# Sliding-window extraction on one core: who loads which half of the channels, and what goes through a staging buffer

## The chip, the cores and the metric

The kernel runs on one core of a Trainium2 chip. The metric is the time of one execution on the device, in microseconds (us); the median of the runs counts. The profile shows one execution of its own, which is named beside its span below.

## The reference

The input x is an array of 16 x 64 x 64 x 64 32-bit floats (batch b, channel c, row, column). From each image, windows of 8 x 8 are cut at a stride of 4, and all are written out, window after window:

```
n_h = (h - window_size) // stride + 1      # 15
n_w = (w - window_size) // stride + 1      # 15
for i in range(n_h):
    for j in range(n_w):
        result[:, i, j] = x[:, :, i*4 : i*4+8, j*4 : j*4+8]
```

Nothing is computed; 16.78 MB are read and, since windows overlap, 58.98 MB are written (16 x 15 x 15 windows of 64 channels x 64 values, 16 KB each).

## The kernel before

**Layout.** The whole input is held in the tile L (line 49). A partition holds one channel half (ch, 32 of the 64 channels), one image b and one quarter q of the rows (16 rows): p = ch x 64 + b x 4 + q, 128 KB each. Images come in two groups, y = 0 (b 0 to 7) and y = 1 (b 8 to 15), so a channel half and a group are 32 partitions. "Lower half" means ch = 0, partitions 0 to 63; "upper half" is ch = 1.

**Loads.** `load` (line 56) brings channels c0 to c1 of one ch, y and q: 8 partitions, every fourth one, with a run of 4 KB per channel. The first FC = 4 channels of each half do not come this way. They are staged: for each ch and q one DMA (line 112) of 16 partitions and 256 KB goes to S[ch], a view of partitions 32 to 95 of the output buffers G2 and G3, which are free at that time. ScalarE's queue issues the four DMAs of the lower half, SP's queue the four of the upper half. Copies at line 126 then bring them to their places in L: two on ScalarE for the lower half, two on VectorE for the upper half, 32 partitions x 4096 elements each. The rest is loaded directly, in the loop at line 114, which goes over y and q (8 steps): in the first six steps SP loads channels 8 to 32 of the lower half (768 KB) and GpSimd channels 4 to 8 (128 KB); in the last two GpSimd loads channels 4 to 32 (896 KB) alone; in all eight GpSimd loads channels 4 to 32 of the upper half (896 KB). That is 16 loads by GpSimd and 6 by SP.

**Output.** There are four output buffers of 128 x 16 KB, taken by turns. Each is filled by copies from L (ScalarE and VectorE; some on VectorE are shuffles with an identity or a next-partition mask), then stored by GpSimd with an indirect DMA of one 16 KB row per partition (`scatter`, line 137). Row numbers come from small index tiles (idx, idx_lo, idx_hi, idx_y0, idx_y1); idx_lo and idx_hi let 16 of the 128 rows fall out of bounds, and those are skipped. There are 29 such stores, and 2 plain ones of SP at the end (line 245).

**Order.** The first three buffers (`part`, line 189) need only y = 0: eight copies each of 32 partitions x 2048 elements, three on ScalarE and five on VectorE, four that read each channel half. Then `part` for y = 1 and `unit` (line 204) follow. A framework derives the waits from which parts of a tile each instruction touches, and may reorder instructions of an engine by its own estimates. It has eight semaphores for the DMAs that SP and ScalarE issue and eight for those of GpSimd; the ninth DMA of either kind waits until the first has landed, and so on.

Of the kernel before, what the change touches and what calls it, by code (L numbers as in the profile page):

```python
# [10 lines left out]
def kernel(  # L11
# [7 lines left out]
    nc = tc.nc  # L19
    P = nc.NUM_PARTITIONS  # L20

    B, C, H, W = x.shape
    Bo, NH, NW, Co, WSo, WSo2 = out.shape
    WS = int(window_size)
# [3 lines left out]
    f32 = mybir.dt.float32  # L28
    i32 = mybir.dt.int32
    ALU = mybir.AluOpType  # L30
    CH = 2
    HQ = P // (B * CH)
    CL = C // CH
    RB = H // HQ
# [3 lines left out]
    HP = P // CH  # L38
    YB = 8
    NY = B // YB  # L40
    QP = YB * HQ
# [4 lines left out]
    gpool = ctx.enter_context(tc.tile_pool(name="gpool", bufs=1))  # L46


    L = lpool.tile([P, CL, RB, W], f32)
# [1 line left out]

    SMALL, HWP = 4, 6

    def load(eng, ch, y, q, c0, c1):
        p0 = ch * HP + y * QP + q
        eng.dma_start(out=L[p0 : p0 + QP - HQ + 1 : HQ, c0:c1, :, :], in_=x_v[ch, y, q, :, c0:c1, :])  # L58
# [43 lines left out]


    NG = 4
    G = [gpool.tile([P, C, WS, WS], f32, name=f"G{n}") for n in range(NG)]
    FC = C * WS * WS // (RB * W)
    S = [g.rearrange("p c r w -> p (c r w)").rearrange("p (c r w) -> p c r w", c=FC, r=RB) for g in G[NG - CH :]]
    x_b = x.rearrange("b (ch cl) (hq r) w -> ch hq b cl (r w)", ch=CH, hq=HQ)
    for ch in range(CH):
        for q in range(HQ):  # L110
            s = S[ch][QP + q : QP + q + (B - 1) * HQ + 1 : HQ]
            (nc.scalar, nc.sync)[ch].dma_start(out=s, in_=x_b[ch, q, :, 0:FC, :])

    for y in range(NY):
        for q in range(HQ):
            hw = y * HQ + q < HWP
            if hw:
                load(nc.sync, 0, y, q, FC + SMALL, CL)
            load(nc.gpsimd, 0, y, q, FC, FC + SMALL if hw else CL)
            load(nc.gpsimd, 1, y, q, FC, CL)  # L120

    for y in range(NY):
        for ch in range(CH):
            f = slice(QP + y * QP, QP + (y + 1) * QP)
            d = slice(ch * HP + y * QP, ch * HP + (y + 1) * QP)
            (nc.scalar.copy, nc.vector.tensor_copy)[ch](out=L[d, 0:FC, :, :], in_=S[ch][f])  # L126

    o_v = out.rearrange("b i j c r w -> (b i j) (c r w)")
    nxt = [min(p + 1, 31) for p in range(32)]

    o_q = out.rearrange("b i j c r w -> i j b (c r w)")

# [27 lines left out]
                copy(out=g[d, cs, 0:ST, :], in_=L[f, :, s * ST : RB, cols])  # L160
                nc.vector.stream_shuffle(out=g[d, cs, ST:WS, :], in_=L[f, :, 0:ST, cols], mask=nxt)  # L161

    act, dve = nc.scalar.copy, nc.vector.tensor_copy
    same = list(range(32))


    def shf(out, in_):
        nc.vector.stream_shuffle(out=out, in_=in_, mask=same)  # L168

    def split(k, other):  # L170
        def both(out, in_):
# [3 lines left out]
        return both  # L175

    mix = split(CL // 4, shf)


# [4 lines left out]
    def tile_():  # L184
        nonlocal at
        at += 1
        return G[(at - 1) % NG]

# [15 lines left out]
    def unit(j, s, copies=(shf, mix)):  # L204
        nonlocal crossed
        g = tile_()
        if s == 0:
            fill(g, 0, 0, j, 0, HP, (act, copies[0]))
            fill(g, 1, 1, j, 0, HP, (act, copies[1]))
            scatter(g, idx, j, s)  # L210
        else:

            turn = 1 - crossed % 2
            crossed += 1
            fill(g, turn, s, j, 0, HP, (act, act))
            fill(g, 1 - turn, s + 1, j, 0, HP, (shf, mix))
            scatter(g, (idx_hi, idx_lo)[turn], j, s)
# [17 lines left out]
    for s in range(2):  # L235
        g = tile_()
        cols = slice(j * ST, j * ST + WS)
        for y in range(NY):
            d = slice(QP + y * QP, QP + (y + 1) * QP)
            for ch in range(CH):  # L240
                f = slice(ch * HP + y * QP, ch * HP + (y + 1) * QP)
# [39 lines left out]
```

## Time and profile before

| | |
|---|---|
| median of 3 runs | 187.62 us (187.61 to 187.77) |
| profiled execution | 187.89 us, its span 186.1 us |
| VectorE, ScalarE, GpSimd busy | 146.8, 146.5, 47.7 us |
| DMA mean | 407 GB/s, 75.81 MB |
| HBM read, written | 16.78 MB, 62.91 MB by the instructions' own account |
| staging DMAs issued | 0.7 to 3.6 us, landed 8.0 to 8.7 us (median) after issue |
| first copy into an output buffer | ScalarE 28.47 us, VectorE 28.49 us |
| first store issued, last | 42.14 us, 175.3 us |

In the profile's page, DMA digits give the mean busy share of the 16 DMA engines in 40 slices (a 9 is 90% or more). Queue q0 is GpSimd's (software), q1 is SP's and q10 is ScalarE's (hardware). A queue's row has its packets, its MB and the time that its packets took as a share of the 16 engines' time in the window. In rows in order of time the first number is the start, the second the duration, both in us; what stands in brackets is the idle time before and what ended it. POOL is GpSimd, ACT ScalarE, DVE VectorE.

### The profile page before, as it was taken

The numbers are of one execution on the slowest core, as the hardware profiler recorded it, in microseconds if no ns is written. First come the engines' busy times: TensorE is split into PE (matmuls) and PEld (weight loads), VectorE is DVE, ScalarE is ACT, GpSimd is POOL, SyncE is SP. The second block draws the span as 40 slices with busy tenths as digits, with TensorE's granted clock in tenths as the row PEclk, the third lists the DMA queues.
The fourth block names the chain that finished last, engine by engine and source line by source line (L and its number), as shares of the span: only waits on it lengthen the run. The fifth ranks groups of instructions, "written<-read, shape, count | busy, mean of one in ns | idle before, by whom it ended". The sixth has DMA issues, their size and how long they took to land.

```text
span 186.1 us, 575 instructions
## 1 busy us (share of the span) xinstructions
DVE 146.8 (79%) x205; ACT 146.5 (79%) x96; POOL 47.7 (26%) x50
## 2 busy tenths in 40 slices
DVE  5045008999998969799999999999999999998600
ACT  0069108997999989988899999998998899999600
POOL 7405222006335341422222222222222222223000
DMA  5999999999999999999999999999999999999994
GB/s 165 359 402 403 399 401 400 381 385 424 433 440 423 431 433 430 433 430 433 424 435 419 433 426 423 433 412 433 398 444 396 444 419 409 440 409 433 409 447 204
DMA packets 11300, 75.81 MB, mean 407 GB/s; under 512 B 3600, under 2 KB 3600, under 8 KB 7696
## 3 DMA queue, kind: packets, MB, share of 16 engines
q0 software_dynamic: 9296, 66.86, 86.6%
q1 hardware_dynamic: 1680, 7.86, 10.6%
q10 hardware_dynamic: 320, 1.05, 1.8%
q14 instruction: 4, 0.03, 0.0%
HBM read 16.78 MB, written 62.91 MB: 428 GB/s over the span
## 4 chain that ended last, share of the span: by engine, by line
DMA 41%; DVE 37%; issue 8%; ACT 5%; POOL 2%; ACTq 1%; POOLq 0%; DVEq 0%; PEldq 0%
DVE G L168 16%; DMA out_dram<-G,idx 14%; DMA out_dram<-G,idx_y 13%; DMA L<-in_x_dram 13%; DVE G L161 11%; DVE G L196 10%; ACT G L243 3%; POOL L L58 2%; ACT G L158 1%; ACT G L172 1%; ACTq L276 0%; DVE G L158 0%; POOLq L138 0%; POOL pi L69 0%; POOL out_dram L138 0%
## 5 line engine op out<-in xcount | busy, mean ns | idle before, releaser
L158 ACT COPY G<-L 64x2048 f32<-64x2048 f32 x46 | 87.2, 1896 | 5.8 <-DMA out_dram<-G,idx 3.7
L168 DVE STREAM_SHUFFLE G<-L 64x1024 f32<-64x1024 f32 (+4 forms) x39 | 53.0, 1358 | 1.2
L196 DVE COPY G<-L 32x2048 f32<-32x2048 f32 x30 | 36.6, 1220 | 14.9 <-DMA L<-in_x_dram 12.1
L196 ACT COPY G<-L 32x2048 f32<-32x2048 f32 x18 | 33.9, 1896 | 11.5 <-DMA L<-in_x_dram 10.4
L161 DVE STREAM_SHUFFLE G<-L 64x1024 f32<-64x1024 f32 x30 | 38.4, 1280 | 0.0
L138 POOL DMA_INDIRECT out_dram<-G,idx_y x6 | 10.7, 1776 | 26.7 <-DVE G L196 16.3
L58 POOL DMA_DIRECT2D L<-in_x_dram x16 | 11.9, 760 | 19.5 <-DMA L<-in_x_dram 19.0
L138 POOL DMA_INDIRECT out_dram<-G,idx_lo x8 | 7.7, 963 | 30.9 <-DVE G L161 12.0
L138 POOL DMA_INDIRECT out_dram<-G,idx x8 | 10.4, 1295 | 18.1 <-ACT G L158 9.3
L138 POOL DMA_INDIRECT out_dram<-G,idx_hi x7 | 6.7, 962 | 26.6 <-DVE G L161 19.0
L126 DVE COPY L<-G 32x4096 f32<-32x4096 f32 x2 | 4.6, 2284 | 8.2 <-DMA G<-in_x_dram 8.2
L172 ACT COPY G<-L 64x256 f32<-64x256 f32 (+2 forms) x21 | 10.2, 484 | 0.5
L126 ACT ACT_TABLE_LOAD x1 | 1.3, 1283 | 10.8 <-DMA G<-in_x_dram 10.8
L158 DVE COPY G<-L 64x2048 f32<-64x2048 f32 x6 | 7.3, 1222 | 0.2
L243 DVE COPY G<-L 32x1280 f32<-32x1280 f32 x8 | 6.5, 818 | 0.9 <-DMA out_dram<-G,idx_hi 0.8
L126 ACT COPY L<-G 32x4096 f32<-32x4096 f32 x2 | 7.2, 3604 | 0.0
L243 ACT COPY G<-L 32x768 f32<-32x768 f32 x8 | 6.6, 829 | 0.1
L168 DVE LOAD_MASK_SELECT G<-L x39 | 0.3, 8 | 1.4 <-DMA out_dram<-G,idx_y 1.0
L72 DVE TENSOR_SCALAR tb<-pi 128x1 int32<-128x1 int32 x1 | 0.2, 153 | 1.0 <-POOL pi L69 1.0
L173 DVE COPY G<-L 64x1280 f32<-64x1280 f32 x1 | 0.9, 874 | 0.0
L78 DVE TENSOR_TENSOR th<-tc,tq 128x1 int32<-128x1 int32 x2 | 0.3, 156 | 0.0
L75 DVE TENSOR_SCALAR th<-tc 128x1 int32<-128x1 int32 x2 | 0.3, 154 | 0.0
(21 smaller groups left out, 3.0 us busy)
## 6 DMA issues: line engine op xcount, KB each, us to landing
L<-in_x_dram POOLq DMA_DIRECT2D x10, 896.0 KB, 19.3
L<-in_x_dram SPq DMA_DIRECT2D x6, 768.0 KB
out_dram<-G SPq DMA_DIRECT2D x2, 1024.0 KB, 10.2
G<-in_x_dram ACTq DMA_DIRECT2D x4, 256.0 KB, 8.0
G<-in_x_dram SPq DMA_DIRECT2D x4, 256.0 KB, 8.7
L<-in_x_dram POOLq DMA_DIRECT2D x6, 128.0 KB, 18.2
out_dram<-G,idx POOLq DMA_INDIRECT x8, 13.2
out_dram<-G,idx_lo POOLq DMA_INDIRECT x8, 10.6
```

The lines of the kernel that those rows point to most:

```text
L58: eng.dma_start(out=L[p0 : p0 + QP - HQ + 1 : HQ, c0:c1, :, :], in_=x_v[ch, y, q, :, c0:c1, :])
L75: nc.vector.tensor_scalar(out=d[:, :], in0=a[:, :], scalar1=float(m), scalar2=None, op0=ALU.mult)
L78: nc.vector.tensor_tensor(out=d[:, :], in0=a[:, :], in1=b[:, :], op=op)
L126: (nc.scalar.copy, nc.vector.tensor_copy)[ch](out=L[d, 0:FC, :, :], in_=S[ch][f])
L138: st = nc.gpsimd.indirect_dma_start(out=o_v, out_offset=bass.IndirectOffsetOnAxis(ap=ix[:, 0:1], axis=0), in_=g.rearrange("p c r w -> p (c ...
L158: copy(out=g[d, cs, :, :], in_=L[f, :, s * ST : s * ST + WS, cols])
L161: nc.vector.stream_shuffle(out=g[d, cs, ST:WS, :], in_=L[f, :, 0:ST, cols], mask=nxt)
L168: nc.vector.stream_shuffle(out=out, in_=in_, mask=same)
L172: act(out=out[:, 0:k], in_=in_[:, 0:k])
L173: other(out=out[:, k:], in_=in_[:, k:])
L196: (act if (2 * d + ch) % 3 == 0 else dve)(out=g[d * QP : (d + 1) * QP, ch * CL : (ch + 1) * CL, :, :], in_=L[f : f + QP, :, s * ST : s * S ...
L243: copy(out=g[d, ch * CL + c0 : ch * CL + c1, :, :], in_=L[f, c0:c1, s * ST : s * ST + WS, cols])
```

## The change

The four output buffers become views of one tile GG, so that the staging buffer S can be one run over the last two of them: 8 channels of one half instead of 4 of each. Only the lower half is staged, by ScalarE's queue alone, four DMAs of 512 KB (16 partitions, 8 channels). SP loads channels 8 to 32 of the lower half directly in all eight steps; the first two steps are cut into two loads of 12 channels. GpSimd loads only the upper half, all 32 channels, in each step 4 channels (128 KB) and then 28 (896 KB). The staging copies become two: ScalarE's for y = 0 and a VectorE shuffle with the identity mask for y = 1, 32 partitions x 8192 elements each. The helpers `act`, `dve`, `same` and `shf` move up.

```
-    SMALL, HWP = 4, 6
+    SMALL, TWICE = 4, 2
...
-    G = [gpool.tile([P, C, WS, WS], f32, name=f"G{n}") for n in range(NG)]
-    FC = C * WS * WS // (RB * W)
-    S = [g.rearrange("p c r w -> p (c r w)").rearrange("p (c r w) -> p c r w", c=FC, r=RB) for g in G[NG - CH :]]
+    GF = C * WS * WS
+    GG = gpool.tile([P, NG, GF], f32)
+    G = [GG[:, n].rearrange("p (c r w) -> p c r w", c=C, r=WS) for n in range(NG)]
+    FC = NG * GF // (CH * RB * W)
+    S = GG[:, NG - NG // CH :].rearrange("p n f -> p (n f)").rearrange("p (c r w) -> p c r w", c=FC, r=RB)
...
-    for ch in range(CH):
-        for q in range(HQ):
-            s = S[ch][QP + q : QP + q + (B - 1) * HQ + 1 : HQ]
-            (nc.scalar, nc.sync)[ch].dma_start(out=s, in_=x_b[ch, q, :, 0:FC, :])
+    for q in range(HQ):
+        nc.scalar.dma_start(out=S[QP + q : QP + q + (B - 1) * HQ + 1 : HQ], in_=x_b[0, q, :, 0:FC, :])
...
     for y in range(NY):
         for q in range(HQ):
-            hw = y * HQ + q < HWP
-            if hw:
-                load(nc.sync, 0, y, q, FC + SMALL, CL)
-            load(nc.gpsimd, 0, y, q, FC, FC + SMALL if hw else CL)
-            load(nc.gpsimd, 1, y, q, FC, CL)
-
-    for y in range(NY):
-        for ch in range(CH):
-            f = slice(QP + y * QP, QP + (y + 1) * QP)
-            d = slice(ch * HP + y * QP, ch * HP + (y + 1) * QP)
-            (nc.scalar.copy, nc.vector.tensor_copy)[ch](out=L[d, 0:FC, :, :], in_=S[ch][f])
+            mid = (FC + CL) // 2 if y * HQ + q < TWICE else CL
+            load(nc.sync, 0, y, q, FC, mid)
+            if mid < CL:
+                load(nc.sync, 0, y, q, mid, CL)
+            load(nc.gpsimd, 1, y, q, 0, SMALL)
+            load(nc.gpsimd, 1, y, q, SMALL, CL)
...
+    def shf(out, in_):
+        nc.vector.stream_shuffle(out=out, in_=in_, mask=same)
+
+    for y, copy in enumerate((act, shf)):
+        copy(out=L[y * QP : (y + 1) * QP, 0:FC, :, :], in_=S[QP + y * QP : QP + (y + 1) * QP])
```

More of the change, by code (lines that the diff above doesn't have):

```diff
@@ L104 @@
     NG = 4
-    G = [gpool.tile([P, C, WS, WS], f32, name=f"G{n}") for n in range(NG)]
-    FC = C * WS * WS // (RB * W)
-    S = [g.rearrange("p c r w -> p (c r w)").rearrange("p (c r w) -> p c r w", c=FC, r=RB) for g in G[NG - CH :]]
+    GF = C * WS * WS
[3 more added lines that the diff above has]
+    S = GG[:, NG - NG // CH :].rearrange("p n f -> p (n f)").rearrange("p (c r w) -> p c r w", c=FC, r=RB)
     x_b = x.rearrange("b (ch cl) (hq r) w -> ch hq b cl (r w)", ch=CH, hq=HQ)
-    for ch in range(CH):
-        for q in range(HQ):
-            s = S[ch][QP + q : QP + q + (B - 1) * HQ + 1 : HQ]
-            (nc.scalar, nc.sync)[ch].dma_start(out=s, in_=x_b[ch, q, :, 0:FC, :])
+    for q in range(HQ):
+        nc.scalar.dma_start(out=S[QP + q : QP + q + (B - 1) * HQ + 1 : HQ], in_=x_b[0, q, :, 0:FC, :])
     for y in range(NY):
         for q in range(HQ):
-            hw = y * HQ + q < HWP
-            if hw:
-                load(nc.sync, 0, y, q, FC + SMALL, CL)
-            load(nc.gpsimd, 0, y, q, FC, FC + SMALL if hw else CL)
-            load(nc.gpsimd, 1, y, q, FC, CL)
-    for y in range(NY):
-        for ch in range(CH):
-            f = slice(QP + y * QP, QP + (y + 1) * QP)
-            d = slice(ch * HP + y * QP, ch * HP + (y + 1) * QP)
-            (nc.scalar.copy, nc.vector.tensor_copy)[ch](out=L[d, 0:FC, :, :], in_=S[ch][f])
+            mid = (FC + CL) // 2 if y * HQ + q < TWICE else CL
[4 more added lines that the diff above has]
+            load(nc.gpsimd, 1, y, q, SMALL, CL)
     o_v = out.rearrange("b i j c r w -> (b i j) (c r w)")
     nxt = [min(p + 1, 31) for p in range(32)]
+    act, dve = nc.scalar.copy, nc.vector.tensor_copy
+    same = list(range(32))
+    def shf(out, in_):
+        nc.vector.stream_shuffle(out=out, in_=in_, mask=same)
+    for y, copy in enumerate((act, shf)):
+        copy(out=L[y * QP : (y + 1) * QP, 0:FC, :, :], in_=S[QP + y * QP : QP + (y + 1) * QP])
     o_q = out.rearrange("b i j c r w -> i j b (c r w)")
@@ L161, in fill @@
                 nc.vector.stream_shuffle(out=g[d, cs, ST:WS, :], in_=L[f, :, 0:ST, cols], mask=nxt)
[L163 to L168, printed above, removed]
     def split(k, other):
```

## The prediction

> **What bounds the kernel now.** I read the page first, the DMA rows above the engine rows, then the DMA view in short windows, then the order of time around the first stores.
>
> The page:
>
> ```profile
> span 186.1 us, 575 instructions
> ...
> DMA  5999999999999999999999999999999999999994
> ...
> DMA packets 11300, 75.81 MB, mean 407 GB/s; under 512 B 3600, under 2 KB 3600, under 8 KB 7696
> ...
> q0 software_dynamic: 9296, 66.86, 86.6%
> q1 hardware_dynamic: 1680, 7.86, 10.6%
> q10 hardware_dynamic: 320, 1.05, 1.8%
> ```
>
> The 16 DMA engines are at nine tenths or more from the second slice to the last but one, while VectorE and ScalarE are busy 79% each. So the packets set the time. The DMA view from 37 to 40 us, when only GpSimd's queue (q0) still loads, prices a 4 KB load packet:
>
> ```profile
> DMA packets 294, 1.20 MB, mean 401 GB/s; under 512 B 0, under 2 KB 0, under 8 KB 294
> ...
> q0 software_dynamic: 294, 1.20, 100.5%
> ```
>
> 3.0 us x 16 engines x 1.005 / 294 = 164 ns. From 46.5 to 168 us the same view gives 617 ns for a 16 KB store packet. The 4096 load packets are then 42.0 us of all engines, the 3600 store packets 138.8, the 3600 small ones at some 10 ns 2.3: 183 of the 186.1 us. What is left is the start and the end. A change of loads can only alter packets, holes in the engines' work, and balance between engines.
>
> Balance matters because a load of 8 partitions does not reach all engines. The view from 33.5 to 35 us, with SP's queue (q1) full:
>
> ```profile
> DMA packets 215, 0.59 MB, mean 393 GB/s; under 512 B 71, under 2 KB 71, under 8 KB 215
> ...
> q0 software_dynamic: 145, 0.30, 53.5%
> q1 hardware_dynamic: 70, 0.29, 48.7%
> ```
>
> SP holds 48.7%, never more while it loads alone: eight of sixteen engines. GpSimd's 8-partition loads also use eight, and the page says so by its small packets. q0 has 9296 packets: 29 stores x 128 rows less 240 skipped rows = 3472 of 16 KB, and 9.97 MB of loads = 2432 of 4 KB. That leaves 3392 = 2432 + 240 + 45 DMAs x 16, exactly one small packet beside each 4 KB one. I infer that the eight engines without data get those. Successive GpSimd loads then take the two halves by turns: the small ones go to SP's half ("low"), the large ones to the other ("high"). Per half, in KB without staging: low 6x768 + 6x128 + 2x896 = 7168, high 8x896 = 7168. Balanced.
>
> **The change, part by part.** All terms are against the profiled execution (187.89 us, span 186.1, 1.8 outside it); the median is 187.62, and I add the sum to that, since start and end stay.
>
> *Bytes.* Staging is again 2048 KB over 16 engines, now by ScalarE's four DMAs alone. Low: 8x768 + 8x128 = 7168; high: 8x896 = 7168. Same bytes on each half: 0 us.
>
> *Small packets.* GpSimd's 4 KB packets fall from 2432 to 2048. The high half got 6x32 + 2x224 = 640 small ones and will get 8x32 = 256, 48 fewer per engine; the low half gets 8x224 in both. At 10 ns (10 to 36 us: 59.2% of 416 us of engine time, less 1421 packets at 163 ns, over 1473 small ones) the high half saves 0.45 us. The high half should be the later one at the end: the eight idx_lo stores skip two rows per low engine, the seven idx_hi two per high one, so a high engine stores two packets (1.2 us) more, against 144 more small ones (1.4 us) on a low one and a load end about a microsecond earlier. Bounds: 0, if the low half ends last, and -0.5.
>
> *The first six microseconds.* Before, ScalarE and SP each issue four DMAs of 256 KB over all engines. Three windows, 3.4 to 4, 4.2 to 4.7 and 5 to 5.5 us, show whose turn it is:
>
> ```profile
> q1 hardware_dynamic: 49, 0.18, 81.2%
> ```
>
> ```profile
> q10 hardware_dynamic: 45, 0.16, 82.0%
> ```
>
> ```profile
> q1 hardware_dynamic: 38, 0.15, 75.2%
> ```
>
> The queues are served a DMA at a time, by turns, a new one each 0.8 us, and each has all engines to work on. After the change SP's turns are 8-partition loads that feed the low half alone. The high half then lives on ScalarE's DMAs until GpSimd's first large load, which starts near 5.75 us (its small one fills 4.4 to 5.3). Before, a high engine gets four DMAs x 4 packets = 16 packets, 2.6 us of work, by then. After, it gets 8 from the first ScalarE DMA, and the second comes when it and SP's half load (96 packets) have passed. How the 0.8 us grows with the packets, no row shows. If not at all (issuing costs 617 ns for 64 packets and 677 for 192), the second is in time: 0 us. If in proportion, the next starts at 2.2 + 1.6 + 1.2 = 5.0 us, 8 packets are missing, and the hole is 1.2 us. The engines' starts are spread over 0.5 us of the first DMA, which speaks for proportion; I take +1.0. Against it, 5.75 to 10 us runs at 356 GB/s where 10 to 15 runs at 411: 0.57 us are lost there. With GpSimd's packets waiting on the high half I give back half: -0.3 (bounds 0 and -0.57).
>
> *Staging copies.* Two L126 copies on each engine (ScalarE 2x3.6, VectorE 2x2.3 us) become one ScalarE copy of 8192 elements, 7.2 us, and one VectorE shuffle. The nearest row, 64x2048 at 2.4 us, gives 9.6; bounds 4.6 (at the copy's rate) and 10. Staging lands near 11 to 12 us now; with ScalarE's rows doubled and SP's loads beside them on the low half, I expect 13 to 16, so both end by 26. The engines have nothing until 28.5 us, when the first 32 channels of y=0 land: hidden, 0 us. If staging lands after 19, the excess is late work.
>
> *SP's queue.* Ten loads instead of four staging DMAs and six loads. With eight semaphores the fifth waits for ScalarE's first DMA to land (4 us after issue now); by then 48 packets per low engine, 7.9 us of work, are queued: 0 us.
>
> *GpSimd's queue.* Sixteen loads before and after, at 0.64 us each. One of them beside a VectorE copy:
>
> ```profile
> 11.82 4.60 DVE L126 COPY L<-G 32x4096 f32<-32x4096 f32 x2 [8.17 <-DMA G<-in_x_dram]
> ...
> 14.59 2.60 POOL L58 DMA_DIRECT2D L<-in_x_dram  x2 [7.62 <-DMA L<-in_x_dram]
> ```
>
> The first of the two took 2.07 us, ending just after the copy. [...] But three large loads were still queued for the engines then, so I cost it at 0. The other way, GpSimd's loads land later: their small packets take turns with SP's on the low half, and ScalarE's are longer there, so the last large load of y=0, 30.84 us now, should land near 33. Its readers' turn on VectorE comes with the seventh copy, at 36.0. Hidden by 2.5 us.
>
> *First store.* It issues at 42.14 us, after ScalarE's seventh copy (ends 41.86); the first 16 KB packet runs at 44.8, just as the high half runs out of loads. This is the one place with no slack shown. SP's y=0 loads should land within 1 us of the present, since the low half has the same packets ahead of them: 0 us. Each later microsecond costs one.
>
> *Sum:* -0.45 + 1.0 - 0.3 = +0.25 us: 187.9.
>
> **Rivals.**
>
> *No hole, only gains.* The queues feed faster than I think, or GpSimd's first large load comes sooner. Then -0.45 - 0.3 to -0.57, and part of the hole at the ramp goes: -0.7, 186.9. For: the issue times hardly grow with size. Against: one DMA at a time in three windows.
>
> *A larger hole.* If the turns become by packet, both queues together bring 64 packets per 0.8 us, ScalarE half of them, the high half 20 per us of the 49 it can eat. By 5.75 us it again has 8 packets per engine, 1.3 us short, and ScalarE stays slow afterwards, so nothing is given back: -0.45 + 1.3 = +0.85, 188.5.
>
> *Late first store (slower).* VectorE and ScalarE take the upper channels first, whose loads land at 33, or staging lands after 19. Eleven VectorE copies of 1.24 us from 33 end at 46.7. The high half, out of loads at 44.8, then waits 1.9 us, or 4.6 if issue to first packet always takes today's 2.7. Taking 2.5: 190.1. It decides from a first store issued after about 43. Against: today's store waits for ScalarE's seventh copy though its buffer holds three, so the lower channels of three buffers come first.
>
> *Eight engines (slower).* If GpSimd's loads lie evenly on 16, low has 768 + 128 + 512 = 1408 KB per engine against 1312 before, 96 KB or 24 packets more: 3.9 us, 191.5. [...] But the exact count of small packets and loads that end everywhere between 44.8 and 46.7 us say that GpSimd already evens it out.
>
> **How the numbers follow.** A measurement here can tell 0.2%, 0.37 us, from no change. Forecast 0.45, spread 187.4 to 188.5: 0.28 within 0.2%, 0.15 slower, 0.02 faster. No hole 0.27, faster. Larger hole 0.10, late store 0.11, eight engines 0.07, all slower. Faster 0.29, same 0.28, slower 0.43. The range, 186.8 to 189.4, holds the forecast, no hole and larger hole and leaves out most of the last two.
>
> **What would show it.** Right: small packets near 3200; in 3.5 to 5.5 us DMA below 300 GB/s; shuffle near 9.6 us over by 26; first store issued at 41 to 43; digits of 9 from 46 us on. Wrong: 360 GB/s or more from 3.5 to 5.5 (no hole); a digit below 9 between 40 and 50 us (late store); SP's queue still loading after 47 us (eight engines).

## The result: 1.7% slower, and the profile after

The changed kernel takes 190.96 us (median of 6 runs, 190.88 to 191.01) where the kernel before, run beside it, takes 187.56 us (6 runs, 187.18 to 187.77). The estimated ratio is 1.0174, with a 95% interval of 1.015 to 1.0198 (the two medians alone give 1.0181). That is on the side the chances leaned to, but 1.6 us above the upper end of the range, and of the listed mechanisms only the hole at the start took part, with a small share. The profiled execution took 190.99 us, its span 189.2 us.

The page of the changed kernel, in the rows shown of before:

```profile
span 189.2 us, 574 instructions
...
DMA  5999999999999999999999999999999999999994
...
DMA packets 10884, 75.81 MB, mean 401 GB/s; under 512 B 3184, under 2 KB 3184, under 8 KB 7280
...
q0 software_dynamic: 8528, 65.29, 84.0%
q1 hardware_dynamic: 1776, 8.39, 11.6%
q10 hardware_dynamic: 576, 2.10, 3.3%
```

The same 75.81 MB move, in 416 fewer small packets, and the engines are at nine tenths or more in the same slices. Yet the span is 3.1 us longer. Since the engines hardly stand idle longer than before, packets must have become longer. Which ones shows in the DMA view from 10 to 40 us, before the first store packet in both kernels. Its GB/s row cuts the window into 40 pieces of 0.75 us. The kernel before:

```profile
GB/s 404 415 404 415 415 410 399 426 393 393 388 415 382 426 388 410 383 410 382 421 393 399 388 404 399 404 399 404 388 393 410 404 388 388 362 362 377 421 421 388
DMA packets 4696, 11.98 MB, mean 399 GB/s; under 512 B 1773, under 2 KB 1773, under 8 KB 4696
...
q0 software_dynamic: 3509, 7.37, 64.8%
q1 hardware_dynamic: 1183, 4.61, 38.9%
```

The changed kernel, same window:

```profile
GB/s 415 393 404 410 399 399 399 399 328 289 284 383 394 399 393 410 393 317 273 311 393 393 404 393 393 383 328 284 306 399 399 388 388 399 410 322 284 290 394 393
DMA packets 4076, 11.05 MB, mean 368 GB/s; under 512 B 1379, under 2 KB 1379, under 8 KB 4076
...
q0 software_dynamic: 2754, 5.96, 58.0%
q1 hardware_dynamic: 1139, 4.44, 40.1%
q10 hardware_dynamic: 183, 0.65, 5.5%
```

Four times in these 30 us the rate falls from about 400 to under 290 GB/s, for some 2 us each, although the engines are full (the shares add to 103.6%). The shares price the packets as the prediction did: 480 us of engine time x 1.036, less the small packets at 10 ns, over the 4 KB packets gives 164 ns before (2923 packets, with q0 and q1 at 103.7% together) and 179 ns after (2697). Over 4096 packets and 16 engines, 15 ns more are 3.9 us. Summed packet by packet over the whole trace, the 4 KB packets take 43.1 us of all engines before and 47.2 after (+4.1), the 16 KB store packets 139.0 and 138.0 (-1.0), the small ones 2.1 and 1.9. The first two alone make the 3.1 us of the span; the 0.1 us of the small ones is made up by 0.2 us more of idle time, in which the hole of the first microseconds lies.

Between those spells nothing has changed. From 33.5 to 35 us, the window shown of before:

```profile
q0 software_dynamic: 191, 0.30, 54.0%
q1 hardware_dynamic: 71, 0.29, 49.6%
```

SP holds its eight engines at 24 us x 0.496 / 71 = 168 ns a packet. Inside the last of the four spells, from 36.5 to 37.1 us:

```profile
DMA packets 40, 0.16 MB, mean 273 GB/s; under 512 B 0, under 2 KB 0, under 8 KB 40
...
q0 software_dynamic: 30, 0.12, 76.2%
q1 hardware_dynamic: 10, 0.04, 25.1%
```

Here SP has only a quarter of the engines' time: GpSimd holds as much as 12 engines (76.2% of 16), which I read as its large load on the eight high ones and its small one (128 KB) in half of the time of the eight low ones. And every packet is long: 9.6 us x 0.762 / 30 = 244 ns on q0, 9.6 x 0.251 / 10 = 241 ns on q1. The bytes say more. All 30 packets of q0 go to partitions 64 to 127: 30 x 4096 B in 0.6 us is 205 GB/s, just what the high engines alone bring there at other times (8 x 4096 B / 164 ns = 200 GB/s). So what came on top, four engines' worth, brought hardly more into the upper half, and the lower half got 10 x 4096 B / 0.6 us = 68 GB/s instead of 200. It is the same over a whole spell, though more packets start in its first half microsecond (0.15 MB from 22.5 to 23 us). From 22.5 to 25 us q0 moves 0.52 MB, 208 GB/s, with 11 engines' worth:

```profile
q0 software_dynamic: 205, 0.52, 70.4%
```

**Theory A (foreign writes).** A half of the partitions takes no more than about 200 GB/s, what eight engines bring. Before, each half was written by its own eight engines: GpSimd's small loads ran on the low engines and wrote the lower half. The change keeps them on the low engines but sends them to the upper half, where the high engines already fill the 200 GB/s; then the low engines wait, and with them SP's packets behind. (Every load here writes every fourth partition of a half, so no run tells the half from smaller groups of partitions within it.) **Theory B (totals):** what counts is only the sum of bytes per half, now 9 MB for the upper one (8 x 1024 KB and half of the staging) against 8 MB. **Theory C (pace):** the hole of the first six microseconds or late GpSimd loads cost the time, and long packets are only a sign of waiting.

### The profile page after: what moved, and what is told of

Read it like the earlier page. It is cut to its first block, busy times and chain, and to the rows that moved or that the text cites. A ratio compares the mean times of both kernels' runs of the same rounds, so it can differ in the third digit from the quotient of the medians.

```text
span 189.2 us, 574 instructions
## 1 busy us (share of the span) xinstructions
DVE 151.5 (80%) x205; ACT 146.3 (77%) x95; POOL 46.2 (24%) x50
## 2 busy tenths in 40 slices
DMA packets 10884, 75.81 MB, mean 401 GB/s; under 512 B 3184, under 2 KB 3184, under 8 KB 7280
## 4 chain that ended last, share of the span: by engine, by line
DMA 44%; DVE 33%; issue 7%; ACT 5%; POOL 4%; ACTq 1%; DVEq 0%; POOLq 0%; PEldq 0%
DVE GG L130 16%; DMA L<-in_x_dram 16%; DMA out_dram<-GG,idx_y 15%; DMA out_dram<-GG,idx 13%; DVE GG L165 11%; DVE GG L194 6%; ACT GG L241 3%; POOL L L58 2%; POOL out_dram L142 1%; ACT GG L162 1%; ACT GG L170 1%; ACTq L274 1%; DVE GG L162 0%; POOL pi L69 0%; DVEq L130 0%
## 5 line engine op out<-in xcount | busy, mean ns | idle before, releaser
L162 ACT COPY GG<-L 64x2048 f32<-64x2048 f32 x46 | 87.2, 1896 | 6.6 <-DMA out_dram<-GG,idx 3.0
L130 DVE STREAM_SHUFFLE GG<-L 64x1024 f32<-64x1024 f32 (+4 forms) x39 | 53.0, 1358 | 1.3
L194 DVE COPY GG<-L 32x2048 f32<-32x2048 f32 x30 | 36.6, 1220 | 9.5 <-DMA L<-in_x_dram 4.9
L194 ACT COPY GG<-L 32x2048 f32<-32x2048 f32 x18 | 33.9, 1896 | 9.5 <-issue 4.5
L165 DVE STREAM_SHUFFLE GG<-L 64x1024 f32<-64x1024 f32 x30 | 38.4, 1281 | 0.0
L142 POOL DMA_INDIRECT out_dram<-GG,idx_y x6 | 11.6, 1940 | 23.4 <-DVE GG L194 20.9
L142 POOL DMA_INDIRECT out_dram<-GG,idx_lo x8 | 7.7, 964 | 30.9 <-DVE GG L165 27.2
L142 POOL DMA_INDIRECT out_dram<-GG,idx x8 | 8.6, 1081 | 19.4 <-ACT GG L162 7.6
L170 ACT COPY GG<-L 64x256 f32<-64x256 f32 (+2 forms) x21 | 10.2, 484 | 0.5
L130 DVE STREAM_SHUFFLE L<-GG 32x8192 f32<-32x8192 f32 x1 | 9.2, 9233 | 0.0
## 6 DMA issues: line engine op xcount, KB each, us to landing
L<-in_x_dram POOLq DMA_DIRECT2D x8, 896.0 KB, 22.5
```

Source lines behind the costliest of these rows:

```text
L142: st = nc.gpsimd.indirect_dma_start(out=o_v, out_offset=bass.IndirectOffsetOnAxis(ap=ix[:, 0:1], axis=0), in_=g.rearrange("p c r w -> p (c ...
L162: copy(out=g[d, cs, :, :], in_=L[f, :, s * ST : s * ST + WS, cols])
L170: act(out=out[:, 0:k], in_=in_[:, 0:k])
L194: (act if (2 * d + ch) % 3 == 0 else dve)(out=g[d * QP : (d + 1) * QP, ch * CL : (ch + 1) * CL, :, :], in_=L[f : f + QP, :, s * ST : s * S ...
```

## The experiments

All ratios are to the kernel before on the same chip: 188.17 us in the first series (the first four below), 188.22 in the second (the next four), 187.96 in the third. "Price" is the mean 4 KB load packet that starts between 10 and 40 us, "loads" and "stores" are the 4 KB and 16 KB packets of the whole trace, in us of all 16 engines.

| kernel | median us | ratio (95% interval) | price ns | loads us | stores us |
|---|---|---|---|---|---|
| before (profile) | 187.56 | 1 | 165 | 43.1 | 139.0 |
| after (profile) | 190.96 | 1.0174 (1.015 to 1.0198) | 179 | 47.2 | 138.0 |
| e1_stage_low | 193.68 | 1.0299 (1.0281 to 1.0316) | 186 | 50.1 | 138.1 |
| e2_stage_high | 194.46 | 1.0345 (1.0326 to 1.0364) | 196 | 51.2 | 138.0 |
| e5_small_home | 190.08 | 1.0112 (1.0095 to 1.0128) | 164 | 43.0 | 140.4 |
| e6_before_sp8 | 188.55 | 1.0026 (1.0009 to 1.0043) | 164 | 42.9 | 139.1 |
| e7_small_scratch | 186.82 | 0.9925 (0.9898 to 0.9952) | 165 | 40.3* | 138.1 |
| e8_before_foreign | 195.66 | 1.0389 (1.0358 to 1.042) | 201 | 48.8* | 138.0 |
| e8b_before_home | 188.46 | 1.0018 (1.0001 to 1.0034) | 165 | 40.4* | 139.0 |
| e3_stage_shared | 190.62 | 1.0132 (1.0104 to 1.0161) | 181 | 46.8 | 138.0 |
| e9_before_order | 187.39 | 0.9972 (0.9953 to 0.9992) | 165 | 43.2 | 138.0 |
| e10_change_home | 191.25 | 1.0173 (1.0146 to 1.02) | 165 | 43.1 | 139.4 |
| e11_after_order | 191.29 | 1.0176 (1.015 to 1.0202) | 180 | 47.5 | 138.6 |
| e12_sp8_order | 187.37 | 0.9972 (0.9954 to 0.999) | 164 | 42.7 | 137.9 |

(* 3840 packets of 4 KB; the small loads of these three go in 128 packets of 8064 B, which are not in the sum. Price, loads and stores are each from one profiled execution.)

The diffs below leave two things out: e5, e7, e8 and e8b fill the channels that are left out with zeros on VectorE, and e7, e8 and e8b keep the ten index tiles in one tile to make room.

### Totals or the moment: staging in one half of the partitions

In the changed kernel the staging buffer lies on partitions 32 to 95, half of it in each partition half. These two move it to 0 to 63 and to 64 to 127. The total per half becomes even in the first (8 and 8 MB) and more uneven in the second (6 and 10).

e1_stage_low (e2_stage_high has 64 in place of 0):

```diff
-        nc.scalar.dma_start(out=S[QP + q : QP + q + (B - 1) * HQ + 1 : HQ], in_=x_b[0, q, :, 0:FC, :])
+        nc.scalar.dma_start(out=S[0 + q : 0 + q + (B - 1) * HQ + 1 : HQ], in_=x_b[0, q, :, 0:FC, :])
...
-        copy(out=L[y * QP : (y + 1) * QP, 0:FC, :, :], in_=S[QP + y * QP : QP + (y + 1) * QP])
+        copy(out=L[y * QP : (y + 1) * QP, 0:FC, :, :], in_=S[0 + y * QP : 0 + (y + 1) * QP])
```

> The changed kernel with the staging buffer moved from partitions 32 to 95 to partitions 0 to 63, nothing else. Theory A (foreign writes): each half of the DMA engines has the write path of its own half of the partitions to itself; a packet that the low engines write into partitions 64 to 127, or the high ones into 0 to 63, waits for the other engines' packets there and costs about 0.12 us per engine. The changed kernel has 32 such packets per low engine (GpSimd's small loads), about +4 us. Here the high engines' 32 staging packets become foreign too: another +3 to +4 us, 194 to 195. Theory B (totals): only the sum written into each half of the partitions counts, 9.44 MB upper and 7.34 MB lower in the changed kernel. Here it is 8.39 and 8.39, so the loads end 4 us sooner: 187. Theory C (pace): loads end late because GpSimd's loads are issued late and the high engines have a hole at the start; the place of staging does nothing: 191.

> The changed kernel with the staging buffer moved to partitions 64 to 127. Theory A (foreign writes): now the low engines' 32 staging packets are foreign: +3 to +4 us, 194 to 195. Theory B (totals): 10.5 MB go to the upper half and 6.3 MB to the lower: +5 us, 196. Theory C (pace): 191, no change.

Both became slower, e1_stage_low by 1.2% over the changed kernel's ratio, where theory B had asked for a gain. Theory A's 194 to 195 us held for e2_stage_high; e1_stage_low stayed 0.3 us below it. The DMA view of e1_stage_low from 10 to 40 us:

```profile
GB/s 295 290 284 284 268 290 279 388 399 399 393 410 393 350 284 273 383 399 404 399 388 404 306 295 306 393 404 393 388 388 404 333 279 317 382 388 388 404 404 393
```

To the spells of the small loads comes one at the start, to about 15 us: now high engines write the lower half, with staging packets. From 11 to 14 us:

```profile
q10 hardware_dynamic: 112, 0.41, 51.1%
q1 hardware_dynamic: 55, 0.23, 27.5%
q0 software_dynamic: 108, 0.22, 27.1%
```

Staging (q10) and SP (q1), both bound for the lower half, hold 79% of the engines' time, more than 12 engines' worth, and bring 0.64 MB in 3 us, 213 GB/s. It is not the staging as such: its last packets run until 18.6 us, but from 15.5 to 18.5 us q10 and q1 hold 50% together, eight engines' worth, and the rate is 403 GB/s. The loss comes from the moment in which one half is written by more than its own eight engines, whichever half it is. Totals that come out even later give nothing back. Theory B falls; so does C, whose 191 us were missed by 2.7 and 3.5 us.

### The small loads brought home, or made foreign

e5_small_home leaves staging and all sizes and sends GpSimd's eight small loads to the lower half:

```diff
-            load(nc.gpsimd, 1, y, q, 0, SMALL)
+            p0 = y * QP + q
+            nc.gpsimd.dma_start(out=L[p0 : p0 + QP - HQ + 1 : HQ, 0:SMALL, :, :], in_=x_v[1, y, q, :, 0:SMALL, :])
...
-        copy(out=L[y * QP : (y + 1) * QP, 0:FC, :, :], in_=S[QP + y * QP : QP + (y + 1) * QP])
+        copy(out=L[y * QP : (y + 1) * QP, SMALL:FC, :, :], in_=S[QP + y * QP : QP + (y + 1) * QP, SMALL:FC])
```

> The changed kernel with GpSimd's small loads sent to the lower half of the partitions: they read the same input, but write channels 0 to 4 of the lower half, and the staging copies write channels 4 to 8 alone. Bytes, queues, order and engines are those of the changed kernel. Left out: channels 0 to 4 of the upper half are never in place (zeros), channels 0 to 4 of the lower half hold the wrong input. Theories A and B: nothing foreign is left, and 8.39 MB go to each half: 187 to 187.5, and 4 KB packets back to about 165 ns. Theory C (pace): 191.

The load packets fell back to 164 ns and 43.0 us, as theory A has it, but the time missed its 187 to 187.5. The edit had a second effect: copies of the lower half now wait for the small loads, the first one starts at 30.2 us instead of 28.4, and the first store is issued at 43.87 us. The DMA digits from 44.5 to 46.5 us, 40 pieces of 0.05 us:

```profile
DMA  8997799886899269219419453564299990000000
```

From 45 us on the engines run dry, for 0.4 us in all. Most of the rest is in the store packets (140.4 us against 139.0, on which more below). So this run shows the packets, not the time. e7_small_scratch cuts that tie: the small loads go to a tile T on lower partitions that nobody reads.

```diff
+    T = ipool.tile([P, SMALL, 1008], f32, name="T")
...
-            load(nc.gpsimd, 1, y, q, 0, SMALL)
+            p0 = y * QP + q
+            nc.gpsimd.dma_start(out=T[p0 : p0 + QP - HQ + 1 : HQ, :, :], in_=x_v[1, y, q, :, 0:SMALL, 0:1008])
```

> The changed kernel with GpSimd's small loads sent into a scratch tile on partitions 0 to 63 that nothing reads, so that, other than in the run before with small loads in the lower half, no copy waits for them. Runs are 4032 bytes instead of 4096 for room. Left out: channels 0 to 4 of the upper half (zeros). Theory A (foreign writes): 4 KB packets back to 165 ns as in that run, and now the first store is issued at 42 us or before, ahead of the end of the loads: within 0.4% of the kernel before (ratio 0.996 to 1.004). If the other 1.9 us of that run came not from the late first store but from the rest of the change (staging on one queue, SP alone on the lower half), the ratio stays near 1.01.

It is 0.7% faster than the kernel before, more than expected (0.9925 against 0.996 to 1.004); of the 1.1 us between the two spans the store packets make 1.0 (138.1 against 139.0). Staging, its queue, SP's loads, the hole at the start and both long staging copies are those of the changed kernel, so none of them can be what costs it 1.7%.

The other way round, in the kernel before. e6_before_sp8 first gives SP its 24 channels in all eight steps, so that all small loads are alike:

```diff
-    SMALL, HWP = 4, 6
+    SMALL, HWP = 4, 8
```

> The kernel before with one part of the change alone: SP loads the lower half in all eight steps, not six; GpSimd keeps small loads of the lower half in all eight. Staging as before. Theories A and B: no foreign packet, same bytes per half, 48 fewer small packets per high engine: -0.2 to -0.5 us, 187.1 to 187.4. Theory C: GpSimd's loads, all in pairs that wait for the low engines, are issued later, as in the changed kernel: slower by 1 to 3 us, 189 to 190.

The small packets fall from 3600 to 3232, and nothing is gained, nor is anything like theory C's 1 to 3 us lost. On top of this, e8_before_foreign and e8b_before_home send the small loads to a scratch tile, on the upper or on the lower partitions:

```diff
-            load(nc.gpsimd, 0, y, q, FC, FC + SMALL if hw else CL)
+            p0 = HP + y * QP + q
+            nc.gpsimd.dma_start(out=T[p0 : p0 + QP - HQ + 1 : HQ, :, :], in_=x_v[0, y, q, :, FC : FC + SMALL, 0:1008])
```

(e8b_before_home has `p0 = y * QP + q`.)

> The kernel before with SP in all eight steps, and GpSimd's small loads (same input, same bytes) sent into a scratch tile on partitions 64 to 127, which nothing reads. Left out: channels 4 to 8 of the lower half (zeros). Theory A: 32 foreign packets per low engine, +3 to +4.5 us against its pair on partitions 0 to 63, that is a ratio of 1.016 to 1.024 to the kernel before; 4 KB packets mean 180 ns or more. If only the changed kernel's other parts made foreign writes dear, no difference to its pair.

> The pair of the run with the scratch tile on partitions 64 to 127: the same, with the scratch tile on partitions 0 to 63. Left out: channels 4 to 8 of the lower half (zeros). Theory A: as the kernel before, ratio 0.996 to 1.003, 4 KB packets at 165 ns.

These two differ in nothing but the partitions that 1 MB of loads is written to: 1.0389 against 1.0018, 7.2 us. The GB/s row from 10 to 40 us, of the foreign one:

```profile
GB/s 333 388 377 371 251 344 355 251 284 301 404 410 355 262 317 349 272 256 279 377 394 382 262 273 409 316 251 289 279 410 393 349 273 322 360 273 256 262 377 393
```

and of the home one:

```profile
GB/s 415 420 420 404 410 409 393 404 404 398 393 393 415 388 399 404 393 398 409 398 399 404 383 399 398 414 393 393 393 410 393 404 415 382 409 399 393 404 393 404
```

The direction is as expected, but the size lies far above the 3 to 4.5 us forecast and is about double that of the changed kernel. Here two rows of the scratch tile go in one packet of 8064 B, and the slow spells are longer; whether the larger packets are the reason was not tried.

### The hole at the start

e3_stage_shared lets SP issue two of the four staging DMAs of the changed kernel, so that both queues begin on all 16 engines:

```diff
-        nc.scalar.dma_start(out=S[QP + q : QP + q + (B - 1) * HQ + 1 : HQ], in_=x_b[0, q, :, 0:FC, :])
+        (nc.scalar, nc.sync)[q % 2].dma_start(out=S[QP + q : QP + q + (B - 1) * HQ + 1 : HQ], in_=x_b[0, q, :, 0:FC, :])
```

> The changed kernel with the four staging DMAs issued by ScalarE and SP by turns (q 0 and 2, q 1 and 3) ahead of SP's loads, so that each turn of the two queues in the first 6 us again feeds all engines. The prediction's hole on the high half was +1.0 us with 0.3 given back. If that is right, -0.4 to -0.9 us against the changed kernel: ratio to the kernel before 1.012 to 1.016. If the hole costs nothing, 1.017 as the changed kernel. Foreign packets are the same in both.

The hole is real. The DMA view from 4.5 to 5 us of the changed kernel:

```profile
DMA packets 24, 0.10 MB, mean 197 GB/s; under 512 B 0, under 2 KB 0, under 8 KB 24
...
q1 hardware_dynamic: 24, 0.10, 48.5%
```

and of e3_stage_shared:

```profile
DMA packets 49, 0.20 MB, mean 401 GB/s; under 512 B 0, under 2 KB 0, under 8 KB 49
...
q1 hardware_dynamic: 49, 0.20, 107.8%
```

In the first, SP alone feeds the low half and the high half stands still. Filled, it brings the ratio from 1.0174 to 1.0132 and the span from 189.2 to 188.6 us, so sharing the staging is worth about 0.6 to 0.8 us (the intervals overlap). Of that, 0.3 us is in the load packets (46.8 instead of 47.2), so not all of it is the hole. The load packets stay long, at 181 ns. The hole is a small part of the loss, not its cause.

### A version of the change without foreign writes

e10_change_home keeps the change's staging, SP's queue and copies, and reads the whole input, but GpSimd's small loads bring lower channels and its large ones all upper ones:

```diff
-            load(nc.sync, 0, y, q, FC, mid)
+            load(nc.sync, 0, y, q, FC + SMALL, mid)
...
-            load(nc.gpsimd, 1, y, q, 0, SMALL)
-            load(nc.gpsimd, 1, y, q, SMALL, CL)
+            load(nc.gpsimd, 0, y, q, FC, FC + SMALL)
+            load(nc.gpsimd, 1, y, q, 0, CL)
```

> The changed kernel, with its staging by ScalarE alone, its loads by SP and its two staging copies, but GpSimd's small loads bring channels 8 to 12 of the lower half (SP then loads 12 to 32) and its large ones all 32 channels of the upper half. The whole input is read. Now every large transfer of GpSimd and every small one writes the partition half of its own engines, but the bytes are uneven: a low engine gets 768 + 128 + 128 KB less one quarter of SP's share, a high one 1024 + 128 KB, 32 packets of 4 KB more than in the kernel before. Theory A: packets of 4 KB fall back to 165 to 170 ns for GpSimd (from 188), 43 to 43.5 us of all engines; the high engines' loads end some 5 us late all the same, near 50 us, so the time is 1.010 to 1.025 of before. Theory A wrong: 47 us of load packets stay, and the imbalance comes on top, 1.035 to 1.05.

The DMA view from 16 to 17 us is the counterpart of the spell shown of the changed kernel. Again a small load has half of the time of the low engines:

```profile
DMA packets 100, 0.40 MB, mean 401 GB/s; under 512 B 2, under 2 KB 2, under 8 KB 100
...
q0 software_dynamic: 74, 0.29, 74.0%
q1 hardware_dynamic: 26, 0.11, 26.4%
```

The shares are the same (74 and 26% against 76 and 25%), but a packet takes 164 ns on q0 and 162 on q1 instead of 244 and 241, and the rate is 401 GB/s instead of 273. That engines are shared is no loss; that one half is written by twelve engines' worth of packets is. The time is nevertheless 1.0173, mainly because the other constraint is now broken, the balance of bytes between the engines. From 42 to 47 us:

```profile
DMA packets 304, 1.05 MB, mean 210 GB/s; under 512 B 48, under 2 KB 48, under 8 KB 304
...
q0 software_dynamic: 304, 1.05, 51.5%
```

The low engines have no loads left while the high ones go on alone, to 50.4 us.

### The order of the first copies, before and after

In the kernel before, the store packets sum to 1.0 us more than after: 177 of the 3600 take over 640 ns, against 66. Those over 640 ns make 0.5 of the 1.0 us; the rest is in packets of 612 to 640 ns. Read over the runs, packets over 640 ns were many where the first store was issued shortly ahead of its first packet (their excess over 612 ns, in us of all engines: 1.46 at 2.1 us ahead in e5_small_home, 1.29 at 2.0 in e10_change_home, 0.73 at 2.6 in before, 0.2 to 0.3 at 4.6 to 6.8 in e3_stage_shared, e7_small_scratch, e1_stage_low and after). Theory D: the lead matters. The first three buffers are filled intertwined, so a fixed order, all copies of one buffer ahead of the next one's, gives a longer lead:

```diff
+    behind = []
...
+        mine = []
+        with ExitStack() as order:
+            for ins in behind:
+                order.enter_context(tc.issue_after(ins))
             for d in range(P // QP):
...
+        behind[:] = [] if y else mine
```

> The kernel before with one thing changed: the copies of the first three output buffers are put in order, all eight of the first buffer ahead of those of the second, and so on. Loads and stores are the same. The first store should be issued near 35 us instead of 42.1, while loads still run, so some 10 us ahead of the first moment at which it could be alone on the engines. Theory D (store packets of 16 KB run slow for a while when the first store comes late, beside engines that are about to run out of loads; the summed excess over the usual 617 ns was 1.46 us per engine with a lead of 2.1 us in e5_small_home, 0.73 with 2.4 to 2.7, 0.2 to 0.3 with 4.6 to 6.8): the excess falls from 0.73 to about 0.25 us, ratio to before 0.995 to 0.998. Theory D wrong (the lead has no part in it): 0.999 to 1.002. A gap of the engines later, because the second and third buffer are now late: above 1.004. The 4 KB packets should stay near 43 us of all engines in every case, since no load changes.

> e6_before_sp8 (the kernel before, with SP loading its 24 channels and GpSimd its 4 channels of the lower half in all eight steps, so that no GpSimd load is left that is large and on the lower half) with the same order of the first three buffers as e9_before_order. If the end is set by the excess of store packets alone, as theory D has it: like e9_before_order, 0.995 to 0.998 of before. If fewer small packets on the high half and the order add up: 0.992 to 0.996. If neither counts: 1.000 to 1.004, where e6_before_sp8 was.

> The changed kernel with the same order of the first three buffers. Its first store is issued at 42.1 us already, 6.8 us ahead of its first packet, since its loads last to 50 us. Theory A (GpSimd's small loads use the low engines but write the upper partitions, where the high engines write too, and the packets of all queues stretch while they run): nothing of that changes, so the load packets stay near 47 us of all engines and the ratio to before stays at 1.012 to 1.020. If instead late copies were what costs the changed kernel its time (theory C, pace): an earlier first store brings it to 1.000 to 1.008.

The first store of e9_before_order, in order of time:

```profile
36.37 1.75 POOL L138 DMA_INDIRECT out_dram<-G,idx_y  x1 [3.12 <-DVE G L203]
```

It is issued 5.8 us earlier than before, 8.7 us ahead of its first packet; the excess falls from 0.73 to 0.27 and the stores to 138.0 us. Both ordered versions of the kernel before end at 0.9972, below 1 by their whole intervals, so they beat both kernels, before by 0.3%. Fewer small packets add nothing to it (e12 as e9). On the changed kernel the order does nothing, 1.0176, with the load packets at 180 ns: its loss is not one of late copies. That run also speaks against a plain law for D: its lead is 7.5 us and its excess 0.54. Nor are the slow packets those of the first stores: half of the 177 of before start after 140 us. Why a store packet is slow stays open.

## Why the prediction was wrong, step by step

- **Bytes: failed here.** "Same bytes on each half: 0 us" balanced the engines, and that balance held. It did not ask which partitions an engine writes. Staging and large loads stay home, as they were, but 8 x 128 KB went from home to foreign: +4.1 us measured on the load packets. The row that showed 12 engines at long packets exists only after the change, but the price could have been bounded: eight engines at 164 ns put 200 GB/s into a half, and no window of before has a half written by more of them, so a gain above 200 was unproven. An estimate from these: if a half takes no more, 128 KB from a third of the writers come in at 67 GB/s, in 2.0 us; SP's half of the low engines adds at most 100, so at 300 instead of 400 GB/s that loses 0.5 us, and eight times 3.9 us, against 4.1 measured.
- **Where the half fills:** 200 GB/s go into the upper half with eight engines (at 164 ns a packet) and 205 with the time of twelve, and SP's packets, bound for the free half, take 241 ns on q1 against 168 outside the spells. That these wait behind stalled packets of the engines they share is theory A's reading; what sets the 200 GB/s, and how the delay reaches q1, no run shows.
- **Small packets:** the count was right (3184, "near 3200"), the -0.45 us was not (48 packets of 10 ns would have been 0.48); e6_before_sp8 and e12_sp8_order put it at its upper bound, 0.
- **The first six microseconds:** right in kind, and about right in size: at most 0.6 to 0.8 us by e3_stage_shared, against +1.0 - 0.3. The rate from 3.5 to 5.5 us is 309 GB/s where I had written below 300. Nothing was won back from 5.75 to 10 us: 356 GB/s in both kernels.
- **Staging copies:** right. The shuffle takes 9.23 us (9.6 forecast) and is over by 24.95 us:

```profile
15.72 9.23 DVE L130 STREAM_SHUFFLE L<-GG 32x8192 f32<-32x8192 f32 x1
...
16.95 0.64 POOL L58 DMA_DIRECT2D L<-in_x_dram  x1 [7.16 <-DMA L<-in_x_dram]
...
36.96 1.21 DVE L194 COPY GG<-L 32x2048 f32<-32x2048 f32 x1 [1.07 <-DMA L<-in_x_dram]
...
42.10 2.44 POOL L142 DMA_INDIRECT out_dram<-GG,idx_y  x1 [3.69 <-DVE GG L194]
```

- **GpSimd's queue:** the cover of 2.5 us was used up. The last upper load of y = 0 landed at 36.8 us, not near 33, and its reader in the third row above waited 1.07 us for it. It cost nothing, since the first store was issued on time all the same. The load of the second row was issued beside the shuffle in 0.64 us, where one beside the copy had taken 2.07. What held that one, no run shows; as costed, nothing came of the difference.
- **First store:** issued at 42.10 us, as forecast, but its first packet runs at 48.9. The loads were late (the last ends at 50.0 us instead of 46.0), not the copies. The rival of a late first store therefore did not happen: no digit falls below 9.
- **Eight engines:** SP's queue was still loading after 47 us, the sign named for this rival, and yet it did not happen, since the small packets, and SP's 49.6% outside the spells, show that GpSimd still alternates. The sign was too weak: any slower load gives it. That its 191.5 us lies near the measured 190.96 is chance.
- **Sum:** +0.25 forecast; 4.1 for foreign writes, less 1.0 for store packets, which no step had, make the 3.1 us of the spans (the hole is small beside them). The term that failed is *Bytes*, put at 0.

## What to carry to other kernels

When loads are split over queues, keep two ledgers: bytes per DMA engine, and bytes per half of the partitions in each stretch of time; here 200 to 213 GB/s go into a half, whoever writes. A load of 8 partitions that its queue puts on the other half's engines should go where those engines already write (here 1.0018 instead of 1.0389). If the GB/s row dips while the busy digits stay at 9, divide share by packets: long packets, not missing ones, are the loss (here 244 ns instead of 164).

## What the hardware showed that I had not expected

- Where a destination half is full at 205 GB/s, the 4 KB packets of the engines that meet there take 244 ns instead of 164, and those of another queue on the same engines, bound for the free half, 241 ns.
- 1 MB moved from home to foreign partitions cost 7.2 us in e8_before_foreign against e8b_before_home, 4.1 us of packets in the changed kernel, 3.0 us of load packets in e1_stage_low. The spread is not explained.
- 16 KB store packets have a slow minority that differs with how the kernel started: 177 of 3600 over 640 ns before, 66 after, 349 in e5_small_home. All store packets together differ by 1.0 us between before and after, and these make half of it. An earlier first store left 76 of them in e9_before_order (0.9972), by a mechanism that stays open.
